# Priority for the operations that finish a token tile, residual reads tile by tile, normed tiles in unit slots, and both column halves of a chunk in turn

## The chip, the cores and the metric

The kernel runs on one core of one Trainium2 chip. The metric is the device time of one execution in microseconds (us); the median of several runs is compared. The engines are TensorE (PE in the profile, with its weight loads as PEld), VectorE (DVE), ScalarE (ACT), GpSimd (POOL) and SyncE (SP), which here only issues DMAs.

## The reference

A trunk of two layers over 1024 tokens of width 1024. Layer 0 mixes tokens with a diagonal state-space scan (S5) and a gated linear unit (GLU), layer 1 with a short gated convolution. Each layer goes on with a SwiGLU feed-forward network (FFN, hidden width 2816) and a gated per-layer embedding (PLE, input `p` of width 256). Each part begins with an RMS norm of the residual `h` and ends with an addition to it. Everything is float32.

```python
def reference(x, p, ...):
    h = x
    for i in range(DEPTH):                                  # DEPTH = 2
        hn = rmsnorm(h, norm_mix_g[i])
        if i % 2 == 0:
            mix = s5_mixer(hn, ...)                         # scan, gelu, z @ w_glu, val * sigmoid(gate)
        else:
            mix = shortconv_mixer(hn, ...)                  # (b * conv3(c * v)) @ w_out
        h = h + mix
        gate, up = split(rmsnorm(h, norm_ffn_g[i]) @ ffn_w_in[i])
        h = h + (silu(gate) * up) @ ffn_w_out[i]
        g = sigmoid(rmsnorm(h, norm_ple_g[i]) @ ple_w_gate[i])
        h = h + g * (p[i] @ ple_w_up[i])
    return rmsnorm(h, final_norm_g)
```

## The kernel before

**Precision and products.** Each float32 operand of a product is split into a high and a low part (`split`, L86: a copy on ScalarE, a subtraction on VectorE), and a product is three matmuls (`mm3`, L121: high by high, high by low, low by high; lines L122 to L124). The 1024 tokens are eight tiles of 128, taken in the order 0, 4, 1, 5, 2, 6, 3, 7 (`ORDER`). `h[t]` is a tile's residual, 128 x 1024.

**Stages.** S5 and its scan come first (to about 220 us). Then follow: GLU (`glu`), FFN input and output of layer 0, PLE 0, convolution input and output, FFN input and output of layer 1, PLE 1. There are two kinds of stage:

- *Inner* stages (`ffn_in`, `conv_in`) compute hidden features on all tokens with a seven-product block scheme: `weights_set` (L254) reads two raw weight tiles and forms seven split operands `ws`; `block_product` (L285) multiplies them by seven blocks of the normed, transposed tokens, four of which lie in `ulow` and three in `uhigh` (`moving`). The results go to device memory as `hid`, in chunks of four hidden tiles by one token tile (512 KB), by GpSimd's queue (`store_hidden`).
- *Outer* stages work one token tile at a time. `out_phase` (L322) reads the chunks `ch` of `hid` back and multiplies them by output weights, in groups of hidden tiles whose split weights fit: three groups (8, 8 and 6 hidden tiles) for the FFN, two groups of 4 for the convolution. Weight units lie in `ulow` (`room_low`), `uhigh` (`room_high`) and four extra slots s0 to s3 of the pool `s8` (`room_new`, tile name `w`). In the FFN the first group's eight units lie in `ulow`, the second's in six slots of `uhigh` and in s0, s1, and the third's in s2, s3 and four slots of `uhigh`. In the last group, `last_post(t)` norms a tile as soon as it is done.

**Around a stage.** `outer` (L1027) opens the pools of an outer stage in the room that the inner stage leaves, and at once reads all eight `h[t]` back from device memory (`hdram`, L1033-1034), where `spill` had put them, eight DMAs on SyncE's queue. In `out_phase`, for each tile, the chunks are read (L342), and then for each half of the 1024 columns (`nb`) all hidden tiles of the group are multiplied into one PSUM bank, which VectorE adds to `h[t]` (L350). In the last group ScalarE also sums squares (`square`, L129). The pool of PSUM banks for products (`mm`) has five.

**Norms.** `norm_stat` (L139) adds up the sums of squares on VectorE and takes the power -1/2 on GpSimd. `normed` (L164) scales `h[t]` into a buffer `xn`, TensorE transposes it in two halves (`transposed`, L172, line L177), and the halves are split into `ulow`. `norm_tile` (L183) does this for one tile, between FFN output and PLE. `norm_pair` (L203) does it for tiles `q` and `q + 4` ahead of an inner stage, and forms the seven blocks with four differences (`T1` to `T4`) and seven splits (`put`). Pair 2 (tiles 2 and 6) is normed after tile 3, pair 3 after tile 7, the last.

**Raw buffers.** Weights as read, chunks and `xn` share four buffers r0 to r3, taken in turn (`raw_tile`, L92). A buffer's next use waits for the end of its last.

**Order on the engines.** The program is written as above. A scheduler then lays out each engine's queue by a simulated time line: of the operations that are ready in the simulation, the one that stands first in the program goes first. A block under `tc.high_priority(offset=n)` counts as standing n instructions earlier. On the chip each queue runs in the order so laid out, and operations wait by semaphores.

Of the kernel before, what the change touches and what calls it, by code (L numbers as in the profile page):

```python
# [9 lines left out]
F32 = mybir.dt.float32  # L10
# [3 lines left out]
AF = mybir.ActivationFunctionType  # L14
ALU = mybir.AluOpType
# [3 lines left out]
P = 128  # L19
# [4 lines left out]
def trunk(  # L24
# [7 lines left out]
    nc = tc.nc  # L32
    V, A, G, PE = nc.vector, nc.scalar, nc.gpsimd, nc.tensor

    S, D = x.shape[1], x.shape[2]
# [29 lines left out]
    ORDER = [t for q in range(HT) for t in (q, q + HT)]  # L65
# [3 lines left out]
    h, hpool = {}, None  # L69
# [9 lines left out]
    hdram = dram.tile([T, P, D], F32, name="hd")  # L79
    hid = [dram.tile([T, P, 4, 2, P], F32, name=f"hid{i}") for i in range((NHT + 3) // 4)]  # L80

    def psum(pool=None):
        pool = pool or mm
        return pool.tile([P, 512], F32, name="ps" + pool.name, tag="ps")
# [7 lines left out]
    def raw_tile(i=None, shape=(P, D), dt=F32, name="raw"):  # L92
        if i is None:
            slots.append(slots.pop(0))
        tag = slots[-1] if i is None else f"r{i}"
        return (uhp if tag == "r3" else rawp).tile(list(shape), dt, name=name, tag=tag)
# [24 lines left out]
    def mm3(ps, ahi, alo, bhi, blo, start, stop, more=False):  # L121
        PE.matmul(ps, ahi, bhi, start=start, stop=False, skip_group_check=more)  # L122
        PE.matmul(ps, ahi, blo, start=False, stop=False, skip_group_check=more)  # L123
        PE.matmul(ps, alo, bhi, start=False, stop=stop, skip_group_check=more)  # L124


    squares = {}

    def square(t, cs):  # L129

        if "ms" not in squares:
            squares["ms"] = tiny.tile([P, T, 4], F32, name="ms", tag="ms")
        got = squares.setdefault(t, [])
        junk = t2_tile("junk", BF16, D)
        ms = squares["ms"][:, t, len(got):len(got) + 1]
        A.activation(junk[:, cs], h[t][:, cs], AF.Square, scale=1.0 / math.sqrt(D), accum_out=ms)  # L136
        got.append(ms)

    def norm_stat(t):  # L139
        ms, *more = squares.pop(t)  # L140
        V.tensor_scalar(ms, ms, EPS, None, ALU.add)
        for m in more:
            V.tensor_tensor(ms, ms, m, ALU.add)
        rs = tiny.tile([P, 1], F32, name="rs", tag="rs", bufs=4)
        G.tensor_tensor(rs, ms, mhalf[:, 0:1], ALU.pow)
        return rs
# [14 lines left out]
    def act(kt, t):  # L161
        return act_view(kt, 0, t), act_view(kt, 1, t)

    def normed(t, gb, halves=1):  # L164
        rs = norm_stat(t)
        xn = raw_tile(name="xn")
        for c in range(halves):
            cs = slice(c * D // halves, (c + 1) * D // halves)
            V.scalar_tensor_tensor(xn[:, cs], h[t][:, cs], rs, gb[:, cs], ALU.mult, ALU.mult)
        return xn  # L170

    def transposed(xn, hf, pool=None):  # L172
# [8 lines left out]
        return a.rearrange("p (c j) -> p c j", c=KH)  # L181

    def norm_tile(t, gb):  # L183
        xn = normed(t, gb)
        for hf in range(2):
            pt = by_kt(transposed(xn, hf))
            kts = slice(hf * KH, (hf + 1) * KH)
            split(act_view(kts, 0, t), act_view(kts, 1, t), pt)
# [133 lines left out]
    def out_phase(wout, groups, last_post, following=()):  # L322


        def fetch(ht, room):
            return unit_of(room(), load_raw(wout[ht], "p n -> p n"))

        units = {ht: fetch(ht, room) for ht, room, _ in groups[0]}
        for gi, group in enumerate(groups):
            last = gi == len(groups) - 1  # L330
            todo = [(early, lambda ht=ht, room=room: units.__setitem__(ht, fetch(ht, room)))
                    for ht, room, early in ([] if last else groups[gi + 1])]
            todo = todo or list(following)
            soon, late = [f for early, f in todo if early], [f for early, f in todo if not early]
            for t in ORDER:
                parts = {}
                for ht, *_ in group:
                    if ht // 4 not in parts:
                        parts[ht // 4] = ch = raw_tile(shape=(P, 4, 2, P), dt=F32R, name="ch")
                        of = [x[0] % 4 for x in group if x[0] // 4 == ht // 4]  # L340
                        ks = slice(min(of), max(of) + 1)
                        nc.sync.dma_start(out=ch[:, ks].bitcast(F32), in_=hid[ht // 4][t, :, ks])  # L342
                for nb in range(2):
                    cs = slice(nb * 512, (nb + 1) * 512)
                    ps = psum()
                    for i, (ht, *_) in enumerate(group):
                        ch = parts[ht // 4][:, ht % 4]
                        bhi, blo = units[ht]
                        mm3(ps, ch[:, 0], ch[:, 1], bhi[:, cs], blo[:, cs], i == 0, i == len(group) - 1)
                    V.tensor_tensor(h[t][:, cs], ps, h[t][:, cs], ALU.add)  # L350
                    if last:
                        square(t, cs)
                if soon:
                    soon.pop(0)()
                if last:
                    last_post(t)
            for f in soon + late:
                f()
# [47 lines left out]
    def ple(l, units, post):  # L406
        more, makers = ple_units(l, 1, [room_new(i) for i in range(4)])
        for nb in range(2):
            cs = slice(nb * 512, (nb + 1) * 512)
            if nb == 1:  # L410
                units = more
            for t in ORDER:
                upt = t2_tile("upt")
                nc.sync.dma_start(out=upt, in_=updram[l][:, t, cs])
                last = l == 1 and t == ORDER[-1] and nb == 1
                for c0, c1 in ((0, 256), (256, 512)) if last else ((0, 512),):
                    ps = psum()[:, 0:c1 - c0]
                    for kt in range(KT):
                        bhi, blo = units[kt // 2]
                        mm3(ps, *act(kt, t), bhi[:, kt % 2, c0:c1], blo[:, kt % 2, c0:c1], kt == 0, kt == KT - 1)  # L420
                    A.activation(ps, ps, AF.Sigmoid)
                    V.tensor_tensor(upt[:, c0:c1], ps, upt[:, c0:c1], ALU.mult)
                    hc = slice(nb * 512 + c0, nb * 512 + c1)
                    V.tensor_tensor(h[t][:, hc], upt[:, c0:c1], h[t][:, hc], ALU.add)
                    square(t, hc)
                if nb == 0 and makers:
                    makers.pop(0)()
                if nb == 1:
                    post(t)
# [40 lines left out]
    def glu(post):  # L470
        wg = s5_w_glu[0].rearrange("(kt p) (two n) -> p kt two n", p=P, two=2)
        rooms = [[room_high(i) for i in range(4)], [room_new(i) for i in range(4)],
                 [room_high(i) for i in (4, 5, 0, 1)], [room_new(i) for i in range(4)]]
        for nb in range(4):
            cs = slice(nb * 256, (nb + 1) * 256)
            units = []
            for u in range(KT // 2):
                raw = raw_tile()
                rv = raw.rearrange("p (kt two n) -> p kt two n", kt=2, two=2)
                for k in range(2):  # L480
                    nc.sync.dma_start(out=rv[:, k], in_=wg[:, 2 * u + k, :, cs])
                units.append([a.rearrange("p (kt n) -> p kt n", kt=2) for a in unit_of(rooms[nb][u](), raw)])
            for t in ORDER:
                ps = psum()
                for kt in range(KT):
                    bhi, blo = units[kt // 2]
                    mm3(ps, *act(kt, t), bhi[:, kt % 2, :], blo[:, kt % 2, :], kt == 0, kt == KT - 1)
                sg = t2_tile("sgg")[:, 0:256]
                A.activation(sg, ps[:, 256:512], AF.Sigmoid)
                V.tensor_tensor(sg, ps[:, 0:256], sg, ALU.mult)  # L490
                V.tensor_tensor(h[t][:, cs], sg, h[t][:, cs], ALU.add)
                square(t, cs)
                if nb == 3:
                    post(t)

# [265 lines left out]
    for k in range(8):  # L761
        c0, s0 = cur
        if k >= 2:
            c1, s1 = ew[:, 0, :, k - 2], ew[:, 1, :, k - 2]
# [262 lines left out]
    def outer(name, n=5):  # L1027
        nonlocal hpool, s8, tiny, t2
        hpool, s8, tiny, t2 = opened(f"h{name}"), opened(f"s8{name}"), opened(f"tiny{name}"), opened(f"t2{name}", n)
        pools.extend((hpool, s8, tiny, t2))  # L1030
        squares.clear()
        h_tiles()
        for t in ORDER:  # L1033
            nc.sync.dma_start(out=h[t], in_=hdram[t])

    def ffn_ple(l, last):
        units, makers = ple_units(l, 0, [room_high(i) for i in (4, 5, 0, 1)])
# [52 lines left out]
```

## Time and profile before

| | us |
|---|---|
| runs | 2416.41, 2411.53, 2411.84 |
| median | 2411.84 |
| the profiled execution | 2402.72 |
| its span, first to last instruction | 2400.9 |
| TensorE busy in it | 2257.4 (94%) |
| VectorE busy | 1333.8 (56%) |
| ScalarE busy | 767.3 (32%) |
| GpSimd busy | 162.6 (7%) |

The mean granted clock of TensorE is 0.975 of full speed. The rows of the profile read as "engine line operation out<-in by the program's names, shape, count", with times in us unless ns is said. A group row has its busy time and mean ns behind the first bar, and behind the second the idle time of the engine just before these instructions, with what ended it. `<-DMA ch<-hid` means that the landing of a read of `hid` into `ch` ended the wait. `SPq` is SyncE's queue, a trailing `xn` with a number (x8) a count. A busy TensorE overlaps its matmuls: a row's length (0.39) is the time through the array, and the spacing of starts is the pace. GLU ends at about 404 us, PLE 0 at 1221, the convolution at 1577; the output phases start at about 846 (FFN 0), 1469 (convolution) and 2018 (FFN 1).

### The profile page before, as it was taken

Reading aid. Unit: us, or ns where it says so; the run is one execution under the profiler, and the core shown is the slowest. Engines: PE = TensorE matmul, PEld = TensorE weight load, DVE = VectorE, ACT = ScalarE, POOL = GpSimd, SP = SyncE. Lnnn points to the kernel's source line nnn. Section 1 sums busy time; section 2 is a strip of 40 time slices with the busy share of each in tenths; the row PEclk is TensorE's granted clock in tenths of the full one; section 3 lists DMA queues with packets and bytes.
Section 4 is the critical chain, followed back from the end, with each engine's and each line's share of the span. In section 5 each row is a group of like instructions: output and inputs, shape, how many; then the busy total and the mean of one; then the engine's idle time right before and its main releaser. Section 6 shows DMA issues by size and latency. Waiting matters only on the chain.

```text
span 2400.9 us, 27099 instructions
## 1 busy us (share of the span) xinstructions
PE 2257.4 (94%) x10253; PEld 1841.2 (77%) x10253; DVE 1333.8 (56%) x2246; ACT 767.3 (32%) x1449; POOL 162.6 (7%) x268
## 2 busy tenths in 40 slices
PE   7988998999999989988979999989999998999898
PEld 5776886788888878867858887868888887887677
DVE  7885227766666532134487775486666664212344
ACT  6554224433333311022343332253333332101232
POOL 2110001000000000000000000001000000000000
PEclk8999999999999999999989999989999999999999
DMA  7556102333334364333232325333343336443233
GB/s 244 137 136 171 38 1 99 112 106 114 106 112 115 120 241 140 100 107 106 86 120 88 93 92 205 132 120 115 113 115 106 106 106 245 132 126 128 66 106 110
DMA packets 212978, 288.87 MB, mean 120 GB/s; under 512 B 21360, under 2 KB 152432, under 8 KB 212848
## 3 DMA queue, kind: packets, MB, share of 16 engines
q1 hardware_dynamic: 191520, 212.63, 28.6%
q0 software_dynamic: 20928, 74.47, 10.0%
q8 instruction: 80, 1.31, 0.2%
q14 instruction: 50, 0.41, 0.1%
q10 hardware_dynamic: 400, 0.04, 0.0%
HBM read 190.93 MB, written 79.69 MB: 113 GB/s over the span
## 4 chain that ended last, share of the span: by engine, by line
PE 84%; DMA 7%; DVE 6%; ACT 1%; SPq 1%; issue 1%; POOL 0%; DVEq 0%; POOLq 0%; ACTq 0%
PE psmm L122 27%; PE psmm L123 27%; PE psmm L124 27%; DMA ch<-hid 4%; PE pstr L177 1%; DMA tw<-tmp 1%; DVE gv L913 1%; DVE W L563 1%; DVE ulow L88 1%; DMA h<-hd 1%; DVE tmp L563 1%; ACT ulow L87 0%; DMA wraw<-in_ple_w_up_dram 0%; DMA W<-W 0%; PE pstr L928 0%
## 5 line engine op out<-in xcount | busy, mean ns | idle before, releaser
L122 PE MATMUL psmm<-ulow,ws 128*128 128x512 f32 x896 | 350.9, 393 | 3.2 <-ACT s L297 2.0
L123 PE MATMUL psmm<-ulow,ws 128*128 128x512 f32 x896 | 350.8, 391 | 0.0
L124 PE MATMUL psmm<-ulow,ws 128*128 128x512 f32 x896 | 350.7, 391 | 0.0
L124 PE MATMUL psmm<-uhigh,ws 128*128 128x512 f32 x672 | 265.3, 395 | 0.0
L122 PE MATMUL psmm<-uhigh,ws 128*128 128x512 f32 x672 | 264.9, 394 | 0.0
L123 PE MATMUL psmm<-uhigh,ws 128*128 128x512 f32 x672 | 264.9, 394 | 0.0
L350 DVE TENSOR_TENSOR h<-psmm,h 128x512 f32<-128x512 f32 x128 | 88.1, 690 | 304.6 <-PE psmm L124 304.3
L88 DVE TENSOR_TENSOR ws<-raw,ws 128x512 fp32r<-128x512 f32 x224 | 154.1, 689 | 117.4 <-ACT ws L87 117.3
L87 ACT CAST ws<-raw 128x512 fp32r<-128x512 f32 x224 | 137.7, 620 | 212.7 <-PE psmm L124 210.7
L122 PEld LDWEIGHTS psmm<-ulow,ws 128*128 128x128 f32 x896 | 169.5, 189 | 41.4 <-ACT s L297 3.3
L123 PEld LDWEIGHTS psmm<-ulow,ws 128*128 128x128 f32 x896 | 169.4, 189 | 36.3
L124 PEld LDWEIGHTS psmm<-ulow,ws 128*128 128x128 f32 x896 | 169.2, 189 | 36.1
L87 ACT CAST ws<-st 128x512 fp32r<-128x512 f32 x168 | 104.2, 621 | 205.7 <-PE psmm L124 192.9
L123 PEld LDWEIGHTS psmm<-uhigh,ws 128*128 128x128 f32 x672 | 126.2, 188 | 30.3
L124 PEld LDWEIGHTS psmm<-uhigh,ws 128*128 128x128 f32 x672 | 126.1, 188 | 30.3
L122 PEld LDWEIGHTS psmm<-uhigh,ws 128*128 128x128 f32 x672 | 126.1, 188 | 29.1
L122 PE MATMUL psmm<-ulow,ch 128*128 128x512 f32 x320 | 127.5, 403 | 20.6 <-DMA ch<-hid 20.6
L136 ACT ACTIVATE junk<-h 128x512 bf16<-128x512 f32 (+1 forms) x113 | 64.1, 567 | 257.6 <-DVE h L350 172.3
L319 POOL DMA_DIRECT2D hid<-hs x104 | 78.3, 756 | 904.3 <-DVE hs L88 896.0
L123 PE MATMUL psmm<-ulow,ch 128*128 128x512 f32 x320 | 128.5, 402 | 0.0
L124 PE MATMUL psmm<-ulow,ch 128*128 128x512 f32 x320 | 128.0, 400 | 0.0
L123 PE MATMUL psmm<-uhigh,ch 128*128 128x512 f32 x320 | 127.8, 399 | 0.0
(240 smaller groups left out, 4163.5 us busy)
## 6 DMA issues: line engine op xcount, KB each, us to landing
hid<-hs POOLq DMA_DIRECT2D x104, 512.0 KB, 4.3
ch<-hid SPq DMA_DIRECT2D x96, 512.0 KB, 3.4
raw<-in_ffn_w_in_dram SPq DMA_DIRECT2D x88, 512.0 KB, 4.5
raw<-in_ffn_w_out_dram SPq DMA_DIRECT2D x44, 512.0 KB, 3.6
hd<-h POOLq DMA_DIRECT2D x24, 512.0 KB, 2.9
h<-hd SPq DMA_DIRECT2D x24, 512.0 KB, 8.4
raw<-in_conv_w_in_dram SPq DMA_DIRECT2D x24, 512.0 KB, 3.9
up<-ev SPq DMA_DIRECT2D x32, 256.0 KB, 3.2
```

The lines of the kernel that those rows point to most:

```text
L87: A.copy(hi, src)
L88: V.tensor_tensor(lo, src, hi.bitcast(F32), ALU.subtract)
L122: PE.matmul(ps, ahi, bhi, start=start, stop=False, skip_group_check=more)
L123: PE.matmul(ps, ahi, blo, start=False, stop=False, skip_group_check=more)
L124: PE.matmul(ps, alo, bhi, start=False, stop=stop, skip_group_check=more)
L136: A.activation(junk[:, cs], h[t][:, cs], AF.Square, scale=1.0 / math.sqrt(D), accum_out=ms)
L177: PE.transpose(pt[:, c * P:(c + 1) * P], xn[:, kt * P:(kt + 1) * P], ident)
L319: nc.gpsimd.dma_start(out=hid[ht // 4][half * HT:(half + 1) * HT, :, ht % 4].rearrange("t p l j -> p t l j"), in_=hs.bitcast(F32))
L350: V.tensor_tensor(h[t][:, cs], ps, h[t][:, cs], ALU.add)
L563: V.tensor_tensor(o, a, b, op)
L913: V.tensor_tensor_scan(gv[:, g, 1:P], dec, sv[:, g, 1:P], 0.0, ALU.mult, ALU.add)
```

## The change

Four edits, all in the outer stages:

- The operations from a finished product to the residual (sigmoid, products, addition, sum of squares) and the norm's scaling up to `xn` stand in a block of priority, 100 instructions earlier. In `out_phase`, GLU and PLE alike.
- `outer` no longer reads the eight residual tiles; `out_phase` reads `h[t]` in its first group, after the chunks of tile `t`.
- `norm_tile` puts `xn` into unit slot s0 or s1 (by `t % 2`) instead of the next raw buffer. `norm_pair` still uses raw buffers.
- `out_phase` takes a chunk of up to four hidden tiles for both column halves before the next chunk, with two PSUM banks open, instead of all chunks for one half and then for the other. The additions follow the last chunk's halves.

```diff
--- before.py
+++ after.py
@@ -126,6 +126,9 @@
 
     squares = {}
 
+    def first():
+        return tc.high_priority(offset=100)
+
     def square(t, cs):
 
         if "ms" not in squares:
@@ -161,12 +164,13 @@
     def act(kt, t):
         return act_view(kt, 0, t), act_view(kt, 1, t)
 
-    def normed(t, gb, halves=1):
-        rs = norm_stat(t)
-        xn = raw_tile(name="xn")
-        for c in range(halves):
-            cs = slice(c * D // halves, (c + 1) * D // halves)
-            V.scalar_tensor_tensor(xn[:, cs], h[t][:, cs], rs, gb[:, cs], ALU.mult, ALU.mult)
+    def normed(t, gb, halves=1, xn=None):
+        with first():
+            rs = norm_stat(t)
+            xn = raw_tile(name="xn") if xn is None else xn
+            for c in range(halves):
+                cs = slice(c * D // halves, (c + 1) * D // halves)
+                V.scalar_tensor_tensor(xn[:, cs], h[t][:, cs], rs, gb[:, cs], ALU.mult, ALU.mult)
         return xn
 
     def transposed(xn, hf, pool=None):
@@ -181,7 +185,7 @@
         return a.rearrange("p (c j) -> p c j", c=KH)
 
     def norm_tile(t, gb):
-        xn = normed(t, gb)
+        xn = normed(t, gb, xn=s8.tile([P, D], F32, name="xn", tag=f"s{t % 2}"))
         for hf in range(2):
             pt = by_kt(transposed(xn, hf))
             kts = slice(hf * KH, (hf + 1) * KH)
@@ -340,16 +344,22 @@
                         of = [x[0] % 4 for x in group if x[0] // 4 == ht // 4]
                         ks = slice(min(of), max(of) + 1)
                         nc.sync.dma_start(out=ch[:, ks].bitcast(F32), in_=hid[ht // 4][t, :, ks])
-                for nb in range(2):
-                    cs = slice(nb * 512, (nb + 1) * 512)
-                    ps = psum()
-                    for i, (ht, *_) in enumerate(group):
-                        ch = parts[ht // 4][:, ht % 4]
-                        bhi, blo = units[ht]
-                        mm3(ps, ch[:, 0], ch[:, 1], bhi[:, cs], blo[:, cs], i == 0, i == len(group) - 1)
-                    V.tensor_tensor(h[t][:, cs], ps, h[t][:, cs], ALU.add)
-                    if last:
-                        square(t, cs)
+                if gi == 0:
+                    nc.sync.dma_start(out=h[t], in_=hdram[t])
+                ps = [psum() for _ in range(2)]
+                for j in parts:
+                    mine = [x[0] for x in group if x[0] // 4 == j]
+                    for nb in range(2):
+                        cs = slice(nb * 512, (nb + 1) * 512)
+                        for ht in mine:
+                            ch = parts[j][:, ht % 4]
+                            bhi, blo = (w[:, cs] for w in units[ht])
+                            mm3(ps[nb], ch[:, 0], ch[:, 1], bhi, blo, ht == group[0][0], ht == group[-1][0])
+                        if mine[-1] == group[-1][0]:
+                            with first():
+                                V.tensor_tensor(h[t][:, cs], ps[nb], h[t][:, cs], ALU.add)
+                                if last:
+                                    square(t, cs)
                 if soon:
                     soon.pop(0)()
                 if last:
@@ -418,11 +428,12 @@
                     for kt in range(KT):
                         bhi, blo = units[kt // 2]
                         mm3(ps, *act(kt, t), bhi[:, kt % 2, c0:c1], blo[:, kt % 2, c0:c1], kt == 0, kt == KT - 1)
-                    A.activation(ps, ps, AF.Sigmoid)
-                    V.tensor_tensor(upt[:, c0:c1], ps, upt[:, c0:c1], ALU.mult)
-                    hc = slice(nb * 512 + c0, nb * 512 + c1)
-                    V.tensor_tensor(h[t][:, hc], upt[:, c0:c1], h[t][:, hc], ALU.add)
-                    square(t, hc)
+                    with first():
+                        A.activation(ps, ps, AF.Sigmoid)
+                        V.tensor_tensor(upt[:, c0:c1], ps, upt[:, c0:c1], ALU.mult)
+                        hc = slice(nb * 512 + c0, nb * 512 + c1)
+                        V.tensor_tensor(h[t][:, hc], upt[:, c0:c1], h[t][:, hc], ALU.add)
+                        square(t, hc)
                 if nb == 0 and makers:
                     makers.pop(0)()
                 if nb == 1:
@@ -486,10 +497,11 @@
                     bhi, blo = units[kt // 2]
                     mm3(ps, *act(kt, t), bhi[:, kt % 2, :], blo[:, kt % 2, :], kt == 0, kt == KT - 1)
                 sg = t2_tile("sgg")[:, 0:256]
-                A.activation(sg, ps[:, 256:512], AF.Sigmoid)
-                V.tensor_tensor(sg, ps[:, 0:256], sg, ALU.mult)
-                V.tensor_tensor(h[t][:, cs], sg, h[t][:, cs], ALU.add)
-                square(t, cs)
+                with first():
+                    A.activation(sg, ps[:, 256:512], AF.Sigmoid)
+                    V.tensor_tensor(sg, ps[:, 0:256], sg, ALU.mult)
+                    V.tensor_tensor(h[t][:, cs], sg, h[t][:, cs], ALU.add)
+                    square(t, cs)
                 if nb == 3:
                     post(t)
 
@@ -1030,8 +1042,6 @@
         pools.extend((hpool, s8, tiny, t2))
         squares.clear()
         h_tiles()
-        for t in ORDER:
-            nc.sync.dma_start(out=h[t], in_=hdram[t])
 
     def ffn_ple(l, last):
         units, makers = ple_units(l, 0, [room_high(i) for i in (4, 5, 0, 1)])
```

## The prediction

> **What bounds the kernel now.** I read the page first, then the waits of TensorE, then its matmuls grouped by tiles and shape, then the chain of waits and the timelines at the places these name. From the page, the busy line and two rows of DMA issues (count, size of one, median time from issue to landing):
>
> ```profile
> PE 2257.4 (94%) x10253; PEld 1841.2 (77%) x10253; DVE 1333.8 (56%) x2246; ACT 767.3 (32%) x1449; POOL 162.6 (7%) x268
> ...
> ch<-hid SPq DMA_DIRECT2D x96, 512.0 KB, 3.4
> ...
> h<-hd SPq DMA_DIRECT2D x24, 512.0 KB, 8.4
> ```
>
> TensorE is the bound. The change removes no matmul, so it can only touch the time in which TensorE waits, and what a wait does to its clock afterwards. What TensorE waits for (total, times, longest):
>
> ```profile
> core 0 of [0], span 2400.9 us
> engine line waited for: us in total, times, longest us
> PE psmm L122 <- DMA ch<-hid: 54.6, 19, 7.6
> PE pstr L177 <- DVE xn L169: 35.7, 5, 10.6
> ```
>
> Of 143.5 us idle (2400.9 less 2257.4), 54.6 are waits for `ch`, the stored hidden activations that the output products read back, and 35.7 are transposes of a normed tile waiting for VectorE. Both belong to stages that the change edits. The first splits by the weights that the waiting matmul uses (idle time is the number behind the second bar):
>
> ```profile
> L122 PE MATMUL psmm<-ulow,ch 128*128 128x512 f32 x320 | 127.5, 403 | 20.6 <-DMA ch<-hid 20.6
> ...
> L122 PE MATMUL psmm<-w,ch 128*128 128x512 f32 x192 | 79.4, 414 | 34.0 <-DMA ch<-hid 34.0
> ```
>
> Weights in `ulow` are those of an output phase's first group: three phases, three waits, 20.6 us. Weights in the unit slots (`w`) open the last group of the two FFN output phases: 16 waits, one for each token tile, 34.0 us, a mean of 2.1.
>
> **The residual reads (first group).** SyncE's queue at the start of the first FFN output phase, and TensorE's timeline there:
>
> ```profile
> 843.64 5.86 SPq L1034 DMA_DIRECT2D h<-hd  x8
> 850.47 3.18 SPq L342 DMA_DIRECT2D ch<-hid  x3
> ```
> ```profile
> 856.40 0.40 PE L123 MATMUL psmm<-ulow,ch 128*128 128x512 f32 x1
> 856.64 0.40 PE L124 MATMUL psmm<-ulow,ch 128*128 128x512 f32 x1
> 864.25 0.79 PE L122 MATMUL psmm<-ulow,ch 128*128 128x512 f32 x1 [7.21 <-DMA ch<-hid]
> ```
>
> Eight reads of 512 KB go out ahead of the second tile's chunk. That chunk, issued at 850.47, is used at 864.25: 13.8 us, where a chunk takes 3.4 in the median. TensorE finished tile 0 at 856.6 and stood for 7.2. The change issues the chunks of a tile, then that tile's residual alone. The chunk issued by 850.5 then lands at about 854, ahead of 856.6, and the wait goes; so do the waits at the other two phases. The same 24 reads remain, each now behind its own tile's chunks on SyncE, with the next tile's chunks and a weight load behind it; it needs no ring slot, and the room that it writes was free for all eight by 849.5. What hides it: a tile of this group is 48 matmuls at 0.24 (the first two rows), 11.5 us, and the sum is added only at its end; the slowest view of such a read is the 8.4 us that it takes among seven others. Without that cover it would cost its landing, 3.4 us (the same size as a chunk), on each tile.
>
> After a wait TensorE runs slowly. The windows (length, busy time of PE, PEld, DVE, ACT, POOL, then granted clock, DMA share, GB/s) are the three resumptions, the two last groups, and three stage ends that come below:
>
> ```profile
> 864.25:872.00 7.75, 7.75 (x27) 6.24 (x28) 1.23 (x1) 1.05 (x1) 0.00 (x0) 0.78 0.35 138
> 1492.20:1500.00 7.80, 7.80 (x27) 6.23 (x28) 3.10 (x4) 2.09 (x2) 0.00 (x0) 0.77 0.39 144
> 2036.99:2045.00 8.01, 8.01 (x25) 6.37 (x26) 1.22 (x1) 1.05 (x1) 0.00 (x0) 0.69 0.35 138
> 1031.59:1125.11 93.52, 77.14 (x333) 60.88 (x332) 34.49 (x54) 20.95 (x46) 3.82 (x7) 0.95 0.26 87
> 2205.28:2302.00 96.72, 79.14 (x336) 62.40 (x335) 34.49 (x54) 20.95 (x46) 3.82 (x7) 0.93 0.25 84
> 405.00:419.00 14.00, 3.57 (x19) 3.03 (x18) 12.92 (x23) 7.89 (x17) 1.13 (x2) 0.69 0.37 114
> 1221.00:1241.00 20.00, 5.40 (x27) 4.60 (x27) 16.76 (x28) 8.22 (x17) 2.49 (x6) 0.63 0.42 142
> 1577.00:1591.00 14.00, 3.37 (x21) 3.03 (x20) 11.94 (x22) 8.97 (x18) 1.49 (x2) 0.65 0.49 150
> ```
>
> The share of clock not granted, times the window, is the time lost: 0.22 x 7.75 + 0.23 x 7.80 + 0.31 x 8.01 = 6.0 us for the three starts. Sum of this part: 20.6 + 6.0 = **26.6 us**.
>
> **Normed tiles in unit slots, and the order of a chunk (last group).** The chain of waits inside the last group, and TensorE after one of these waits:
>
> ```profile
> 1064.77 0.89 PE pstr L177 x8
> 1065.68 3.37 DMA ch<-hid
> ```
> ```profile
> 1069.09 0.79 PE L122 MATMUL psmm<-w,ch 128*128 128x512 f32 x1 [2.73 <-DMA ch<-hid]
> 1069.68 0.63 PE L123 MATMUL psmm<-w,ch 128*128 128x512 f32 x1
> 1070.11 0.63 PE L124 MATMUL psmm<-w,ch 128*128 128x512 f32 x1
> ```
>
> Four raw buffers go round in a ring. In the last group a tile takes three of them: two chunks and its normed copy `xn`. So the chunk of the tile after next gets the buffer of an `xn`, which is free only when TensorE has transposed it, and the program has those transposes near the end of the following tile. The chunk's load starts as they end (1065.66 to 1065.68), takes 3.4 us, and TensorE stands. Now `xn` goes to unit slots s0 and s1, whose weights the group before has used up. The ring then carries two chunks of four, loaded a tile ahead: 3.4 us of load against a tile of 36 matmuls at 0.24 and 8 transposes (0.89), 9.5 us. What is late next is the slot of `xn` itself, shared by two tiles in succession; its transposes are done before the second of them ends, so that costs nothing. The clock: 0.05 x 93.52 + 0.07 x 96.72 = 11.5 us; the three rows show it, 0.43 from start to start against 0.24 above.
>
> Of the 16 waits, the two on a group's first tile have another cause: there the chunk's buffer comes behind weight splits, which wait until the group before has read the slots. Taking both column halves of a chunk in turn reads those weights 12 matmuls (2.9 us) earlier, against a wait of 2.1 or so; with several loads at once I count half of these two as left, 2.1 us. Sum: 34.0 + 11.5 - 2.1 = **43.4 us**. The order costs nothing else: the same matmuls on the same banks, two banks open at a time of five.
>
> One rule of the Trainium skill speaks against the 11.5. "TensorE: Matmul & The Clock Gate", section "HAM oscillation — how this bites in real kernels", puts the clock's fall behind idle gaps of more than about 3.4 us; by it no wait of the last groups would slow TensorE, and 11.5 us would stay. The trace does not agree: a wait of 2.73 is followed by matmuls at nearly half speed. I take the rows.
>
> **Priority (stage ends).** In the steady part of a stage nobody waits for these operations (no such row among TensorE's waits), so they move at no cost there, covered by the five banks. What is left are the ends of GLU, of the first per-layer embedding and of the convolution. At GLU's end:
>
> ```profile
> 403.65 0.39 PE L124 MATMUL psmm<-w,ulow 128*128 128x512 f32 x1
> ...
> 408.42 0.40 ACT L489 ACTIVATE sgg<-psmm 128x256 f32<-128x256 f32 x1
> ...
> 411.99 0.42 DVE L490 TENSOR_TENSOR sgg<-psmm,sgg 128x256 f32<-128x256 f32 x1
> ...
> 415.49 1.42 DVE L169 SCALAR_TENSOR_TENSOR xn<-h,rs,gb 128x512 f32<-128x512 f32 x2 [0.75 <-POOL rs L145]
> ...
> 416.82 0.69 DVE L88 TENSOR_TENSOR ws<-raw,ws 128x512 fp32r<-128x512 f32 x1
> ```
>
> The last tile's sigmoid stands 4.4 us behind its matmul, its product another 3.2 behind the sigmoid, because splits of the pair before are ahead in both queues. With priority `xn` can come some 8 us earlier (4.4 + 3.2). But VectorE is nearly full there: 12.92 of 14.00 us, 16.76 of 20.00, 11.94 of 14.00. The next stage's first product also needs the split of its weights (416.82), which stands last in the program; it now finds the nine remaining operations of the last pair ready before it, 9 x 0.69 = 6.2 us. So the end moves by about the time in which VectorE idles: 1.1 + 3.2 + 2.1 = **6.4 us** in all. Bounds for each end: 8 earlier, if TensorE can begin with the first product alone, and 5 later, if the weights fall behind all of it (6.2 less the 1.1 idle); in all from 24 gained to 15 lost. I stay in the middle, since the full queue is what the windows show.
>
> **Sum.** 26.6 + 43.4 + 6.4 = 76.4 us. The profiled execution took 2402.72 us (span 2400.9), 9.1 under the median of the runs shown; it would come to 2326.3. I take the same microseconds off the median: 2411.8 - 76.4 = **2335.4 us**.
>
> **Rivals.** (1) The stage ends give their full bound: TensorE begins the next product on the first block while VectorE still splits the rest. For it: the first of seven products needs one block alone. Against: VectorE's fullness. 17.6 us more: 2317.8.
>
> (2) The chunks stay late in the last group: something else holds the ring or SyncE's order, and half to all of the 43.4 stays. For it: weights of the next stage go through the same ring and queue. Against: only two of them are asked for before the group's end. 2357 to 2379.
>
> (3) Slower than before: the residual read takes the place of the burst. If the order on SyncE puts each read behind a chunk that waits for its ring buffer until the tile's own products end, every addition of a first group waits 3.4 us: 24 x 3.4 = 82 us. It decides once a read is issued later than 3.4 us before its tile's end and the five banks are full. 2335.4 + 82 = 2417. Against: a tile of 11.5 us, and banks for two tiles more.
>
> (4) The slow clock of the last groups is not the waits' doing, as the page's rule would have it: 11.5 stay, 2346.9. Against: the slow matmuls start right at a wait.
>
> (5) Priority does not change an engine's order, or changes it for the worse by the bound: 2342 to 2357.
>
> **How the numbers follow.** Forecast 0.55, rival (1) 0.15, (2) 0.10, (3) 0.04, (4) 0.06, (5) 0.10. The predicted time is the forecast's. The range reaches from a little under rival (1), 2312, up to 2370, which holds (4), (5) and the milder half of (2); outside lie the worse half of (2), rival (3), and both sides' mishaps, some 0.15 to 0.2. A measurement of this kernel tells about 0.2%, 4.8 us, from no change. Only (3), and something like it that I have not seen, ends slower: 0.04; within 0.2% needs gains and losses to meet by chance: 0.02; faster 0.94.
>
> **What would show it.** Right: among TensorE's waits no `ch` row of more than some 5 us in all; reads of `h` spread over the first group, each landed before its addition; transposes in the last group no longer followed by a chunk's load in the chain; a granted clock near 1 there; tiles of about 9 us. The row of transposes waiting for `xn` shrinks, but VectorE's fullness at the stage ends stays and first products wait for `ws` or `ulow` instead. Wrong: a wait of additions for `h<-hd` (rival 3), `ch` waits of 2 us that stay (rival 2), or stage ends shorter by 5 us and more each (rival 1).

## The result, and the profile after

The changed kernel takes 2357.67 us (median of 4 runs, 2355.86 to 2359.43) against 2412.45 (4 runs of the kernel before beside it, 2411.53 to 2416.41): a ratio of 0.977, 95% interval 0.9753 to 0.9787. It is faster by 54.8 us. The profiled executions differ by less, 2402.72 against 2359.43, 43.3 us. Before's profiled execution lies below all its unprofiled runs here (lowest 2405.41 of 34 runs beside the experiments); why is open. Steps are compared by the profiles, whole kernels by the runs.

TensorE's waits after (total, times, longest), and the two groups of matmuls that waited for chunks:

```profile
PE pstr L181 <- DVE xn L173: 36.0, 5, 10.7
PE psmm L122 <- DMA ch<-hid: 19.9, 7, 4.6
```
```profile
L122 PE MATMUL psmm<-ulow,ch 128*128 128x512 f32 x320 | 128.4, 401 | 10.8 <-DMA ch<-hid 10.8
...
L123 PE MATMUL psmm<-uhigh,ch 128*128 128x512 f32 x320 | 126.3, 395 | 1.0 <-DVE uhigh L88 1.0
...
L122 PE MATMUL psmm<-w,ch 128*128 128x512 f32 x192 | 77.7, 405 | 9.2 <-DMA ch<-hid 9.2
```

Waits for chunks fell from 54.6 to 19.9: in the first groups from 20.6 to 10.8, in the last groups from 34.0 to 9.2. The wait for `xn` at the stage ends did not shrink (35.7, now 36.0).

The whole gain lies in the three output phases. Their windows, each from its first product (the convolution's from the first one behind the last product of its input stage) to its last (length, busy time of PE, PEld, DVE, ACT, POOL, then granted clock, DMA share, GB/s), before and after:

```profile
845.67:1127.36 281.69, 258.10 (x1113) 208.19 (x1112) 74.59 (x104) 35.67 (x62) 5.88 (x10) 0.97 0.38 129
1478.53:1576.37 97.84, 92.02 (x410) 74.71 (x409) 51.81 (x84) 24.10 (x51) 10.97 (x17) 0.97 0.46 167
2018.04:2303.89 285.85, 260.69 (x1113) 209.60 (x1112) 75.12 (x105) 35.66 (x62) 5.88 (x10) 0.96 0.38 127
```
```profile
848.02:1112.59 264.57, 255.21 (x1113) 207.74 (x1113) 76.13 (x105) 36.55 (x63) 5.87 (x10) 0.97 0.42 143
1463.40:1556.97 93.57, 90.84 (x410) 73.27 (x409) 51.92 (x85) 24.15 (x51) 10.25 (x17) 1.00 0.49 176
1997.65:2260.34 262.69, 253.88 (x1113) 206.48 (x1112) 74.89 (x104) 36.46 (x62) 5.88 (x10) 0.98 0.42 144
```

Together 665.4 before and 620.8 after: 44.6 us less, and all else in the span is 1.2 longer. Of the 44.6, 33.7 is idle time (length less busy, 54.6 to 20.9); the other 10.9 is the same matmuls done in less busy time (610.8 to 599.9), the pace that TensorE loses after a wait. What is left shows in the windows after: 20.9 us are still idle, and in the two FFN phases the granted clock is still 0.97 and 0.98.

**The wait left in the first groups.** SyncE's queue at the start of the first FFN output phase of the changed kernel, and TensorE there:

```profile
846.86 0.90 SPq L348 DMA_DIRECT2D h<-hd  x2
848.97 0.32 SPq L346 DMA_DIRECT2D ch<-hid  x1
849.34 3.57 SPq L348 DMA_DIRECT2D h<-hd  x6
853.94 1.59 SPq L346 DMA_DIRECT2D ch<-hid  x2
```
```profile
864.59 0.40 PE L124 MATMUL psmm<-ulow,ch 128*128 128x512 f32 x1
869.58 0.80 PE L122 MATMUL psmm<-ulow,ch 128*128 128x512 f32 x1 [4.59 <-DMA ch<-hid]
```

In the program each residual read stands behind its own tile's chunks; on the queue six of them still go out in a row, at 849.34. They need no ring buffer, so they are ready at once, while the chunks written ahead of them wait for theirs. The chunk issued behind them at 853.94 is used at 869.58, 15.6 us later. The burst was moved by one chunk, not spread.

**The wait left in the last groups.** There is now one wait at each group's second tile, 4.24 and 4.35 us. SyncE's queue and TensorE at the first of them:

```profile
1032.82 0.38 SPq L100 DMA_DIRECT2D raw<-in_ple_w_gate_dram  x1
1033.29 0.42 SPq L100 DMA_DIRECT2D raw<-in_ffn_w_out_dram  x1
1039.01 1.50 SPq L346 DMA_DIRECT2D ch<-hid  x3
```
```profile
1041.02 0.40 PE L124 MATMUL psmm<-uhigh,ch 128*128 128x512 f32 x1
1045.66 0.80 PE L122 MATMUL psmm<-w,ch 128*128 128x512 f32 x1 [4.24 <-DMA ch<-hid]
```

A weight of the next stage (`ple_w_gate`) takes a ring buffer at 1032.82. The next chunks are issued at 1039.01, some 2 us before TensorE needs the first of them. Both places are tried below.

### The profile page after: what moved, and what is told of

Same layout as the page of the kernel before. It is cut to its first block, busy times and chain, and to the rows that moved or that the text cites. A ratio compares the mean times of both kernels' runs of the same rounds, so it can differ in the third digit from the quotient of the medians.

```text
span 2357.5 us, 27090 instructions
## 1 busy us (share of the span) xinstructions
PE 2247.0 (95%) x10253; PEld 1835.7 (78%) x10253; DVE 1331.9 (56%) x2246; ACT 765.5 (32%) x1449; POOL 163.1 (7%) x268
## 3 DMA queue, kind: packets, MB, share of 16 engines
q0 software_dynamic: 20928, 74.47, 10.2%
## 4 chain that ended last, share of the span: by engine, by line
PE 85%; DMA 6%; DVE 5%; ACT 1%; SPq 1%; issue 1%; POOL 0%; DVEq 0%; POOLq 0%; ACTq 0%
PE psmm L122 27%; PE psmm L124 27%; PE psmm L123 27%; DMA ch<-hid 2%; PE pstr L181 1%; DMA raw<-in_ffn_w_out_dram 1%; DMA tw<-tmp 1%; DVE W L575 1%; DVE gv L925 1%; DMA h<-hd 1%; DVE tmp L575 1%; DVE ulow L88 1%; DVE uhigh L88 1%; PE pstr L874 0%; DVE raw L575 0%
## 5 line engine op out<-in xcount | busy, mean ns | idle before, releaser
L122 PE MATMUL psmm<-ulow,ch 128*128 128x512 f32 x320 | 128.4, 401 | 10.8 <-DMA ch<-hid 10.8
L87 ACT CAST uhigh<-raw 128x1024 fp32r<-128x1024 f32 x36 | 37.2, 1049 | 278.9 <-PE psmm L124 136.7
```

Of the source, the lines that this page charges most:

```text
L87: A.copy(hi, src)
```

## The experiments

The first four kernels ran beside one another (kernel before: 2408.0), the next four (2409.82), and the last four (2408.27). The changed kernel itself ran with none of them, beside a kernel before of 2412.45; a difference from it below is therefore good to some 4 us. The changed kernel without priority ran with the second four and took 2357.97. The first four are the kernel before with one of the change's four edits alone, as in the diff above.

**Normed tiles in unit slots alone.**

```diff
-        xn = normed(t, gb)
+        xn = normed(t, gb, xn=s8.tile([P, D], F32, name="xn", tag=f"s{t % 2}"))
```

> The kernel before with one part of the change alone: the normed tile of norm_tile goes to a unit slot. Theory A (the ring is what makes the last groups wait): 14 of the 16 waits go with the slow clock behind them, so TensorE's wait of w-weight products for ch falls from 34.0 to under 12 us and the time by 30 to 40 us; what stays is one wait of about 4 us near the start of each last group, as in the changed kernel (9.2 us in all there). Theory B (the halves' order does it, by freeing the first chunk's buffer half a tile earlier): less than 10 us faster. The waits at the start of the output phases (20.6 us) and at the stage ends (35.7) stay under both.

2361.53 us, ratio 0.9801 (0.9777 to 0.9824): 46.5 us less.

```profile
L122 PE MATMUL psmm<-ulow,ch 128*128 128x512 f32 x320 | 127.2, 403 | 22.8 <-DMA ch<-hid 22.8
...
L122 PE MATMUL psmm<-w,ch 128*128 128x512 f32 x192 | 76.9, 400 | 4.5 <-DMA ch<-hid 4.5
```

Of the last groups' 16 waits only the two on the first tiles are left, 2.17 and 2.29 us. The gain is more than the 30 to 40 us expected, and the waits of some 4 us expected near the groups' starts are not there: the second tile waits for nothing, although `ple_w_gate` is read at the same place (1032.77). One line brings most of what the whole change brings.

**Residual reads tile by tile alone.**

```diff
-        for t in ORDER:
-            nc.sync.dma_start(out=h[t], in_=hdram[t])
...
+                if gi == 0:
+                    nc.sync.dma_start(out=h[t], in_=hdram[t])
```

> The kernel before with one part alone: the residual is read in the first group, each tile's read behind its chunks in the program. Theory A (the queue is laid out by what is ready, so the reads, which need no ring buffer, still go out in a burst; only one chunk gets ahead of the last six): the wait of ulow-weight products for ch falls from 20.6 to about 11, and the time by 8 to 14 us. Theory P (the prediction: the reads go out one by one and the wait goes): it falls to under 3 and the time by about 26 us.

2403.85 us, ratio 0.998 (0.997 to 0.999): 4.2 us less.

```profile
L122 PE MATMUL psmm<-ulow,ch 128*128 128x512 f32 x320 | 127.1, 403 | 10.2 <-DMA ch<-hid 9.4 <-DVE h L352 0.8
...
L122 PE MATMUL psmm<-w,ch 128*128 128x512 f32 x192 | 80.9, 421 | 40.1 <-DMA ch<-hid 40.1
```

The first groups' waits halve, as in the changed kernel, but the last groups, where nothing was edited, wait 40.1 instead of 34.0. The edit must be read in both rows: 10.4 gained, 6.1 given back, so that the time fell by less than the 8 to 14 us expected. Some 2 us of such a difference may be the spread between two traces: with priority alone, which moves no read, the same rows have 22.7 and 36.3.

**Both halves of a chunk in turn alone** (the loop over `parts` and `nb` of the diff).

> The kernel before with one part alone: both column halves of a chunk in turn. Theory A: the chunk's buffer comes free earlier, but in the last groups the next load waits for the normed tile's buffer all the same, so only the two waits on a group's first tile shrink: 0 to 6 us faster. Theory B (the order is what removes the last groups' waits): 20 us and more.

2395.14 us, ratio 0.9946 (0.9928 to 0.9965): 12.9 us less.

```profile
L122 PE MATMUL psmm<-ulow,ch 128*128 128x512 f32 x320 | 130.1, 407 | 22.7 <-DMA ch<-hid 22.7
...
L122 PE MATMUL psmm<-w,ch 128*128 128x512 f32 x192 | 79.3, 413 | 27.5 <-DMA ch<-hid 27.5
```

Here the last groups wait only at every second tile, some 3.3 us, right behind the transposes. By the program a tile's second chunk is now needed 12 matmuls (2.8 us at 0.23) later than before, which would hide it. The first tiles' waits shrink as well. Neither expectation had the size right.

**Priority alone, and the changed kernel without priority.**

```diff
     def first():
-        return tc.high_priority(offset=100)
+        return ExitStack()
```

> The kernel before with one part alone: the priority blocks. Theory A (at the stage ends the last tile's operations are not ready in the layout's simulation before the splits ahead of them have been queued, so priority hardly moves them): within 3 us of before, and the wait of transposes for xn stays at 35 to 37 us. Theory P (the prediction: the ends get shorter by what VectorE idles there): about 6 us faster, with that wait at 30 or less. Rival: the order gets worse, 3 us and more slower.

> The changed kernel without the priority blocks. If priority does nothing here: within 3 us of the changed kernel, the wait for xn at 35 to 37 us. If it does what the prediction put on it: about 6 us slower than the changed kernel.

Alone 2410.32 us, ratio 1.0004 (0.999 to 1.0017). Without it 2357.97, ratio 0.9782 (0.976 to 0.9803), where the whole change has 2357.67. Priority does nothing to the time. The end of GLU in the changed kernel is one of the places where it was to act. TensorE's last matmul there, the last tile's product, its addition and its scaling on VectorE, and a window of 14 us over it:

```profile
406.32 0.39 PE L124 MATMUL psmm<-w,ulow 128*128 128x512 f32 x1
```
```profile
413.45 0.42 DVE L502 TENSOR_TENSOR sgg<-psmm,sgg 128x256 f32<-128x256 f32 x1
...
416.19 0.42 DVE L503 TENSOR_TENSOR h<-sgg,h 128x256 f32<-128x256 f32 x1
...
418.15 1.41 DVE L173 SCALAR_TENSOR_TENSOR xn<-h,rs,gb 128x512 f32<-128x512 f32 x2 [0.75 <-POOL rs L148]
```
```profile
407.67:421.67 14.00, 3.58 (x19) 3.05 (x18) 12.92 (x23) 7.87 (x17) 1.13 (x2) 0.71 0.36 113
```

From the last matmul to the scaling it is 11.8 us, as before (403.65 to 415.49). The product now stands ahead of three `uhigh` splits and not of one; those three then stand ahead of the addition. VectorE does 12.92 us of work in the window, exactly as before.

**The residual read behind its tile's last chunk** (the changed kernel, with the read bound to its place in the queue).

```diff
-                        nc.sync.dma_start(out=ch[:, ks].bitcast(F32), in_=hid[ht // 4][t, :, ks])
+                        read = nc.sync.dma_start(out=ch[:, ks].bitcast(F32), in_=hid[ht // 4][t, :, ks])
                 if gi == 0:
-                    nc.sync.dma_start(out=h[t], in_=hdram[t])
+                    with tc.issue_after(read.ins):
+                        nc.sync.dma_start(out=h[t], in_=hdram[t])
```

> The changed kernel, with each residual read held in SyncE's queue behind its own tile's last chunk (an order edge, no wait), so that the reads really go out one by one. If the burst is what is left of the first groups' waits: the wait of ulow-weight products for ch falls from 10.8 to under 3 us and, with the slow clock behind it, the time by 10 to 16 us (to 2342 to 2348). Rival (the read takes the burst's place): additions wait for h, or ch waits stay, and the time is the changed kernel's or more.

2341.14 us, ratio 0.9713 (0.9696 to 0.973): 16.5 us less than the changed kernel, a little more than expected. SyncE's queue, and the group that waited 10.8 us:

```profile
841.87 0.42 SPq L349 DMA_DIRECT2D h<-hd  x1
843.82 6.19 SPq L346 DMA_DIRECT2D ch<-hid  x2
850.06 1.01 SPq L349 DMA_DIRECT2D h<-hd  x1
851.16 2.21 SPq L346 DMA_DIRECT2D ch<-hid  x1
```
```profile
L122 PE MATMUL psmm<-ulow,ch 128*128 128x512 f32 x320 | 126.4, 395 | 0.0
```

Reads and chunks alternate, and the first groups' waits for chunks are 0.0 instead of 10.8. A read does stand 6.2 us behind a chunk that waits for its buffer (843.82 to 850.06), which is the mechanism of the slower rival; it costs nothing here, since no row of TensorE waits for an addition.

**The next stage's weights from the third tile on** (the changed kernel, with the early PLE loads moved in the last groups).

```diff
-                if soon:
+                if soon and not (last and t in ORDER[:2]):
                     soon.pop(0)()
```

> The changed kernel, with the two early loads of the embedding's gate weights asked for from the third tile of the last group on, not from the first. If these two loads, which go through the same ring, make the second tile's chunk late: the wait of w-weight products for ch falls from 9.2 to under 2 us and the time by 8 to 13 us. Rival: the weight splits of the last group itself hold the ring, and the wait stays; or the embedding's first products now wait for their weights, and nothing is gained.

2341.97 us, ratio 0.9716 (0.9698 to 0.9734): 15.7 us less than the changed kernel, more than the 8 to 13 expected. SyncE's queue at the same place, and the group that waited 9.2 us:

```profile
1026.71 5.83 SPq L346 DMA_DIRECT2D ch<-hid  x3
1032.63 0.38 SPq L100 DMA_DIRECT2D raw<-in_ffn_w_out_dram  x1
1037.22 6.75 SPq L346 DMA_DIRECT2D ch<-hid  x3
1045.48 0.38 SPq L100 DMA_DIRECT2D raw<-in_ple_w_gate_dram  x1
```
```profile
L122 PE MATMUL psmm<-w,ch 128*128 128x512 f32 x192 | 75.9, 396 | 0.0
```

The load of `ple_w_gate` follows the chunks, and the last groups wait 0.0 for chunks instead of 9.2. So the two loads are part of the cause; the kernel with the unit slots alone, where the same loads make no tile wait, shows that another part of the change is needed too, and no run says which. The gain is the 9.2, the 1.0 for `uhigh`, and the slow clock behind the two waits. The changed kernel's windows at the two resumptions:

```profile
1045.66:1053.50 7.84, 7.84 (x22) 6.17 (x23) 1.23 (x1) 1.05 (x1) 0.00 (x0) 0.61 0.16 50
2193.90:2201.70 7.80, 7.48 (x24) 5.97 (x25) 1.23 (x1) 1.05 (x1) 0.00 (x0) 0.69 0.17 56
```

The clock not granted is 0.39 x 7.84 + 0.31 x 7.80 = 5.5 us; 9.2 + 1.0 + 5.5 = 15.7, the gain measured. That it fits so closely is chance, since the runs of each kernel spread by some 4 us.

**The last tile first at the stage ends** (the changed kernel). The splits of the pair before are held on VectorE and ScalarE behind the last tile's addition and sum of squares, which priority had not done. Pair 2 is still normed after tile 3, but its splits come after tile 7; the main lines of the edit:

```diff
             if t == T - 1:
+                with tc.issue_after(done[0].ins), tc.issue_after(done[1].ins):
+                    pair(HT - 2, done[2])
                 pair(HT - 1)
```

> The changed kernel, with the splits of pair 2 held behind the last tile's addition and sum of squares in VectorE's and ScalarE's queues (order edges), which gives the order that the priority was to give. Theory V (VectorE is nearly full at the ends): xn comes 5 us and more earlier at each end, but the first products then wait for their weights' or blocks' splits, and the whole is 2 to 9 us faster than the changed kernel. Rival Q (only the order in the queue holds the ends): 15 to 24 us faster. Third: no gain or slower, when the held splits are themselves what the first products need.

2354.52 us, ratio 0.9769 (0.9748 to 0.9791): 3.2 us less than the changed kernel, which is within the spread of the two (their runs overlap). The waits for `xn` fall from 36.0 to 4.9, but others come: 10.2 for the copy `b` (L220), 6.6 and 2.3 for `ws`. The first 30 us from GLU's last product on, and the whole way to the last product of the FFN input stage, of the changed kernel and of this one:

```profile
406.55:847.80 441.25, 430.15 (x1873) 350.96 (x1871) 299.59 (x469) 168.56 (x288) 32.66 (x44) 0.99 0.39 115
...
406.55:436.55 30.00, 18.90 (x83) 15.16 (x82) 27.17 (x47) 17.94 (x33) 1.13 (x2) 0.83 0.38 116
```
```profile
403.87:846.96 443.09, 435.23 (x1881) 353.89 (x1880) 301.09 (x472) 169.64 (x290) 32.64 (x44) 0.98 0.39 116
...
403.87:433.87 30.00, 22.14 (x84) 16.23 (x83) 28.38 (x49) 18.31 (x34) 1.13 (x2) 0.72 0.42 125
```

TensorE begins the next stage's products 6.1 us after GLU's last instead of 14.0, 8 us earlier, and yet has 84 matmuls behind it after 30 us instead of 83, and the stage ends 1.8 us later, not earlier. The 30 us show where the 8 us went. TensorE idles 3.2 us less (7.86 against 11.10), but is busy 3.2 us longer (22.14 against 18.90) with one matmul more, at a granted clock of 0.72 instead of 0.83: it starts early, waits again, and runs slowly. VectorE is busy 28.38 of the 30.00 us, so what the first products wait for could hardly come sooner. Which of the two would have been enough to take the gain is not separated. The same windows behind all three stage ends add up to 1130.1 us in the changed kernel and 1132.2 here, with 7.7 less idle and 9.7 more busy. The 3.2 us of the runs are thus not found at the stage ends; waits for chunks are 17.2 instead of 19.9.

**Both repairs together** (residual reads bound, next weights later).

> The changed kernel with both repairs: the residual read behind its tile's last chunk, and the PLE loads from the third tile on. Theory A (the two late arrivals are separate: reads ahead of the first groups' chunks, weight loads ahead of the last groups' second chunk): the gains of 16.5 and 15.7 us add, 2322 to 2329 us, and waits of matmuls for chunks come to less than 1 us in all. Theory B (what one repair lets start earlier collides elsewhere, as the reads moved by themselves made the last groups' waits rise from 34.0 to 40.1): 2333 to 2341 us, with 4 us or more of chunk waits left.

2325.06 us (2323.68 to 2325.97), ratio 0.9651 (0.9635 to 0.9667): 32.6 us under the changed kernel, where the two gains give 16.5 + 15.7 = 32.2. They add, within the 4 us to which such differences hold. The three output phases:

```profile
843.93:1093.65 249.72, 249.72 (x1114) 204.04 (x1112) 75.14 (x105) 36.38 (x62) 5.86 (x10) 1.00 0.44 152
1444.79:1535.00 90.21, 90.21 (x410) 73.45 (x409) 51.91 (x84) 24.14 (x51) 10.24 (x17) 1.00 0.52 187
1976.23:2226.91 250.68, 249.96 (x1113) 203.97 (x1112) 75.83 (x105) 36.36 (x62) 5.87 (x10) 1.00 0.45 151
```

They take 590.6 us, with 0.7 idle and a granted clock of 1.00 throughout. So 589.9 is the work at full clock, and the change's own phases had 30.2 us of waits and slow clock left. Of three more kernels each alters this one in one respect.

**Both repairs, chunks in the old order.**

> The kernel with both repairs, its chunks in the old order (one column half over the whole group, then the other). Theory A (the order of halves only covers a chunk that is late; with none late it is worth nothing): within 3 us of the kernel with both repairs, chunk waits under 1 us. Theory B (it also takes away the entry wait of a group's first tile, 2.2 and 2.3 us in the run with the unit slots alone, because the second chunk of a tile is needed later): 4 to 8 us slower than with both repairs, with first-tile waits of 2 us each in the last groups.

2334.27 us, ratio 0.9691 (0.9677 to 0.9705): 9.2 us slower, as theory B has it but beyond its 8. The order of the halves keeps a worth of its own, which is the last groups' first tiles:

```profile
1021.18 0.40 PE L124 MATMUL psmm<-w,ch 128*128 128x512 f32 x1
1024.96 0.47 PE L122 MATMUL psmm<-w,ch 128*128 128x512 f32 x1 [3.39 <-DMA ch<-hid]
```

This wait and its like of 2.23 us in the other FFN phase give 5.6; behind each of them seven or eight matmuls start 0.43 us apart instead of 0.23, some 3 us in all.

**Both repairs, normed tiles in the ring.**

> The kernel with both repairs, its normed tiles back in the ring that the chunks come through. Theory A (a normed tile in the ring holds back a later tile's chunk, whatever else is mended): 25 to 45 us slower than with both repairs, matmuls of the last groups wait 22 to 40 us for chunks, at every tile after the second. Theory B (the ring was short only because the PLE loads shared it with the normed tiles; without these loads at the first tiles it suffices): under 15 us slower, waits under 12 us.

2364.32 us, ratio 0.9818 (0.9803 to 0.9832): 39.3 us slower.

```profile
L122 PE MATMUL psmm<-w,ch 128*128 128x512 f32 x192 | 79.6, 415 | 25.0 <-DMA ch<-hid 25.0
```

Of the 25.0 us most is in six waits of 3.2 to 4.4 us, the first at each group's second tile and the others two or three tiles apart, much as with the halves alone. The ring is short by the normed tile itself, whether the PLE loads share it or not.

**Both repairs, the last tile first at the stage ends.**

> The kernel with both repairs and, besides, pair 2's splits held behind the last tile's addition and sum of squares on VectorE and ScalarE. Theory V (at the stage ends VectorE is nearly full, so an earlier last tile is paid back by splits that come later): 1 to 5 us faster than with both repairs, as it was 3.2 us faster without them. Theory P (the order of the stage end is the limit): 6 us or more faster.

2326.36 us, ratio 0.9658 (0.9643 to 0.9672): no gain, where 1 to 5 us was expected. With the chunks' waits gone nothing of the 3.2 us is left, which agrees with the windows above: they were not the stage ends'.

## Why the prediction was right, and where it was not

The forecast was 2335.4, the result 2357.67: inside the range, in the direction with the chance of 0.94, and 22 us short of the gain forecast. By profiles the sum was 76.4 and 43.3 came, 33.1 less. Both repairs close most of that, and show which steps were at fault. Of the signs named for a right forecast, two came fully, transposes without a chunk's load behind them and, with them, tiles of about 9 us; but waits for chunks were 19.9 us and not 5, six reads still went out in a row, and the wait for `xn` did not shrink.

**The mechanism of the last groups was right (43.4).** The chunk of the tile after next came behind a normed tile in the ring. That was shown from both sides: the slots alone bring 46.5 us, and taking them out of the mended kernel costs 39.3. The step that failed is the reason against rival (2): "only two of them are asked for before the group's end". In the changed kernel two are enough. They go through the ring at the first two tiles, and the group pays one wait of 4.3 us and the clock behind it; without them 15.7 us go in two groups. Rival (2) named the cause, but only half of the shortfall is its own: that the result lies at its lower end, 2357, is chance.

**The residual reads (26.6) came out at less than half.** The cause was right, since binding the read to its place takes the first groups' waits to 0.0. The step that failed is "The change issues the chunks of a tile, then that tile's residual alone": true of the program, not of the queue. The scheduler puts first what is ready first, and a read that needs no ring buffer is ready long before the chunks written ahead of it. The waits went from 20.6 to 10.8, and 16.5 us stayed behind.

**The order of the halves was undersized.** It was given the share that removes half of two first-tile waits. In the changed kernel one is gone and the other is 0.57, and measured alone the order is worth 12.9, in the mended kernel 9.2. In the kernel before, with its normed tiles in the ring, it also leaves long waits only at every second tile. The edits overlap: alone they give 46.5 + 4.2 + 12.9 = 63.6 us with priority at nothing, together 54.8.

**Priority (6.4) gave nothing.** The step that failed is "With priority `xn` can come some 8 us earlier": it came 11.8 us behind the last matmul, as before. Why the laid-out order still has the splits ahead is not shown. The bound from VectorE's fullness was the right reading, and the number taken from it was not: of the 1.08 us in which VectorE idles (14.00 less 12.92), 0.75 is the wait for `rs` in the chain itself, which a new order leaves there. Even an order that starts TensorE 8 us earlier gained nothing. The forecast also left out that TensorE would run at a lower clock between such waits (0.72 against 0.83). Rival (1) falls with that, and of rival (5) the milder half holds: no gain from priority, and no loss.

**The slow clock (6.0 + 11.5) was the waits' doing.** With the waits gone the granted clock of the output phases is 1.00, and busy time of the same matmuls falls from 610.8 to 589.9 us, 20.9 against the 17.5 forecast. Rival (4) falls.

Taken together, the first two parts were forecast at 70.0 us; the output phases give 665.4 - 590.6 = 74.8 once nothing is late. The size of what was there was read rightly. What was wrong is that the change would take all of it.

Not settled: why the last groups wait longer when only the residual reads are moved (40.1 against 34.0, of which some 2 may be the spread of traces), what besides the early loads makes the second tile wait, and the 11.5 us between the profiled difference and that of the runs.

## What to carry to other kernels

Where a scheduler orders a queue by readiness, a transfer that needs no buffer overtakes every one that does, so read the queue, not the program, and bind a transfer to the one that it should follow. Where loads share a ring, list every user of it at the place of the wait, the next stage's loads too: the normed tiles cost some 40 us here, two early weight loads in each of two groups 16 us. Before giving operations priority, compare the busy time of their engine with the window; where it is full, earlier for one is later for the next. Then look whether the order changed where it should, for the same chain can come out as long as before.

## What the runs showed of the hardware

A wait of about 2 us can be enough to slow TensorE. In the kernel with the unit slots alone there is one wait in the last group of the first FFN phase, of 2.17 us, and TensorE comes out of it at 0.43 us from start to start for some 3 us, then goes on at 0.23:

```profile
1031.77 0.54 PE L122 MATMUL psmm<-w,ch 128*128 128x512 f32 x1 [2.17 <-DMA ch<-hid]
...
1032.53 0.63 PE L124 MATMUL psmm<-w,ch 128*128 128x512 f32 x1
1032.96 0.63 PE L122 MATMUL psmm<-w,ch 128*128 128x512 f32 x1
...
1035.49 0.40 PE L122 MATMUL psmm<-uhigh,ch 128*128 128x512 f32 x1
```

The Trainium skill, "TensorE: Matmul & The Clock Gate", section "HAM oscillation — how this bites in real kernels", asks for no idle gaps over about 3.4 us. The 2.17 us here does not agree with that as a safe limit. Not every wait does it: of the eight in the last group of the first FFN phase of the kernel before, 1.2 to 2.7 us long, three were followed by such a stretch, and in the mended kernel with its normed tiles in the ring a wait of 3.22 us (1105.49) was not. So these runs give no length of wait that is safe or unsafe by itself. A wait of 2 us is best priced at itself and up to 1.7 us more, some eight matmuls at 0.2 us lost each.
